# Head norms of a recurrence and a neighbourhood attention: one Newton chain each, and k's columns first

## The chip, the cores and the metric

The kernel runs on one core of one Trainium2 chip. The metric is the device time of one execution in microseconds, as the median over several runs. Three runs of the kernel before took 2517.57, 2526.06 and 2529.08 us; the median is 2526.06.

## What is computed

The reference is a stack of blocks over 512 tokens of 1024 features (a gated recurrence with a convolution mixer, a conformer convolution, two cross attentions, two convolutional feed-forwards), then a second block: a mixer of two branches and a mixture of experts. The change lies in the second block's mixer:

```python
h = rmsnorm(x, norm1_g)
p = h @ w_in                                   # 1024 x 5504 columns
p_rwkv, q, k, v, gate_logits = split(p)
# branch 1: a recurrence in both directions over 8 heads of 64
p = p + mu_prev * (prev - p) + mu_next * (nxt - p)         # token shift
r, k, v, wl_f, wl_b, al_f, al_b, gl = split(p)
kk = heads(k * k_k)
kk = kk * rsqrt(sum(kk * kk, -1) + 1e-12)      # head norm of the recurrence's keys
# ... decays, rates, the state's recurrence, group norm, bonus
# branch 2: attention over a window of a 8 x 64 grid, 8 heads of 64
q = q * rsqrt(mean(q * q, -1) + 1e-6) * q_gain * 64 ** -0.5
k = k * rsqrt(mean(k * k, -1) + 1e-6) * k_gain
# ... scores with a bias, softmax, values
x = x + (g_a * y_a @ w_o_rwkv + g_b * y_b @ w_o_na) @ w_out
```

So there are three head norms: of the recurrence's keys, and of q and k of the attention. Each is a sum of squares over the 64 features of a head, for every token and head, then an inverse square root.

## The kernel before

Activations lie with features on the 128 partitions and the 512 tokens along the free axis; a tile of 128 x 512 holds two heads. Large products are made of 128 x 128 weight blocks. Each block is three matmuls of 512 columns (`mm3`, lines 524 to 526), because the weights and the activations are split into a rounded part and a rest: ScalarE rounds the weights (`whi`, L353) and VectorE or GpSimd takes the rest (`wlo`, L356). The blocks come from DRAM in chunks of 1 MB on SP's queue, in the order in which `plan` lists them, and `Stream.block` asserts that they are used in just that order. The accumulators in PSUM are five `acc` tiles and three `aux` tiles.

`w_in` has 43 column tiles of 128: 0 to 3 are r, 4 to 7 k and 8 to 11 v of the recurrence; 12 holds the decay's and 13 the rate's low-rank input, 14 the gate's; 15 to 18, 19 to 22 and 23 to 26 are q, k and v of the attention; 27 to 42 are the two branches' gates. `W_IN` (lines 83 to 92) lists them in the order of their computation. The first four (`AHEAD`) are accumulated together while the norm before them is still under way. The inner generator `columns` computes them one by one: it yields after the first four of a column's eight blocks (`begin`) and again when its epilogue is issued, so a column is two steps. A recurrence column is shifted (`shifted`: a multiply, a scaling on ScalarE and two scalar_tensor_tensor on VectorE) and kept in one of the tiles of `self.x`, whose own contents were written to DRAM just before. An attention column is multiplied by the token norm (L1241) and written to DRAM (`nq0` to `nv3`). A gate column goes through a tanh and to DRAM too.

The stages interleave by hand. First 10 steps of `columns` run. Then `prep` runs for the four pairs of heads p = 0 to 3: decays, products with the keys, Gram matrices. At each of its ten yields the strings `PREP` and `INVS` say how many steps of the columns and of `inverse(0)` are issued in between. Then `inverse(1)` runs with columns (`SOLVE`) and pieces of the attention (`NEAR`). Last come the 32 slots of the recurrence (`chunk`, eight chunks for each pair), between which `GATE` and `REST` issue what is left of the columns and of the attention. Within these, each engine has a queue whose order is fixed when the program is built; a step that is not ready can be set behind a later one there, but on the chip each engine works through its own queue in order.

The head norms. `by_head` (L625) sums the squares of a tile for each head with four matmuls against a 128 x 2 selector, which gives a 128 x 8 tile with tokens on the partitions. `rsqrt` (lines 604 to 619) turns it into the inverse square root by a Newton iteration: a multiply-add, two integer operations for the first guess and three rounds of three instructions, 12 on VectorE, each on 128 x 8 and each waiting for the one before. `head_rms` does both and spreads the result back over the features (L635, eight matmuls). In `prep`, ScalarE scales the keys (L1402) and squares them (L1403); after the first yield `head_rms` follows and VectorE multiplies the keys by its result (L1473). In the attention's `start(p)`, once for each pair, q and k are read back from DRAM and squared (L1292, L1297); q's chain gives `rq` with one more instruction for the factor 0.125 (L1294), and k's goes through `head_rms` into the keys (L1300). `scores` uses `rq` as a scale for each token.

Of the kernel before, what the change touches and what calls it, by code (L numbers as in the profile page):

```python
# [8 lines left out]
F32 = mybir.dt.float32  # L9
F32R = mybir.dt.float32r  # L10
I32 = mybir.dt.int32
AF = mybir.ActivationFunctionType
ALU = mybir.AluOpType
# [3 lines left out]
P = 128  # L17
# [8 lines left out]
EPS = 1e-6  # L26
# [21 lines left out]
AHEAD = 4  # L48
# [31 lines left out]


OTHERS = list(range(15, 27)) + [14] + list(range(27, 43))
W_IN = [12, 13, 4, 0, 8]
for _p, _n in enumerate(BETWEEN):
    _h = [5 + _p, 1 + _p, 9 + _p] if _p < 3 else []
    _m = len(_h) + _n
    for _i in range(_m):
        if len(_h) and (_i + 1) * 3 // _m > _i * 3 // _m:
            W_IN.append(_h.pop(0))
        else:  # L90
            W_IN.append(OTHERS.pop(0))
W_IN += OTHERS


def plan():
# [52 lines left out]
    for m in (0, 8, 4, 12):  # L148
# [5 lines left out]
    blocks("w_in_2", 0, range(8),  # L154
           W_IN, AHEAD)
    blocks("w_o_na_2", 0, range(4), range(8))
# [288 lines left out]
class Kernel:  # L445
# [158 lines left out]
    def rsqrt(self, ps, n, scale, eps=EPS):  # L604
# [13 lines left out]
            r = o  # L618
        return r

    def by_head(self, sq):

        ps = self.aux()
        for j in range(4):
            self.nc.tensor.matmul(ps[:, 2 * j:2 * j + 2], sq[:, j * P:(j + 1) * P], self.c("sel"),  # L625
                                  start=True, stop=True)
        return ps[:, :8]

    def head_rms(self, sq, scale=1.0 / 64, eps=EPS):

        r = self.rsqrt(self.by_head(sq), 8, scale, eps)
        ps = self.aux()
        for j in range(4):
            for e, h in enumerate(HALF):
                self.nc.tensor.matmul(ps[h, j * P:(j + 1) * P],  # L635
                                      r[:, 2 * j + e:2 * j + e + 1].to_broadcast([P, 64]), self.idn,
                                      start=True, stop=True)
        return ps
# [496 lines left out]
    def final_norm(self):  # L1135


        nc = self.nc
        gf = self.v("final_norm", 0, DT)
        gg = self.C.tile([P, DT], F32, name="gg")  # L1140
        nc.vector.tensor_mul(gg, gf, self.v("norm1_g_2", 0, DT))
        xs = [self.split(t, scale=gg[:, i:i + 1]) for i, t in enumerate(self.x)]
        among = self.aheads(xs, "w_in_2", 0, range(8), (12, 13, 4, 0))
        for _ in range(6):
            next(among)
        r = self.rsqrt(self.by_token(*self.total(self.x, True, ends=ENDS)), 4, 1.0 / D)

        q = self.M.tile([P, 8], F32, name="rs", bufs=12)[:, :4]
        u = self.M.tile([P, 8], F32, name="rs", bufs=12)[:, :4]
        nc.vector.tensor_mul(q, r, r)  # L1150
        nc.vector.tensor_mul(u, q, self.by_token(*self.total(self.x, True, gf, ENDS)))
        r2 = self.rsqrt(u, 4, 1.0 / D)
        rr = self.M.tile([P, 8], F32, name="rs", bufs=12)[:, :4]
        nc.vector.tensor_mul(rr, r, r2)
        for _ in among:
            pass
        rb = self.M.tile([P, S], F32, name="rb", bufs=2)
        nc.vector.tensor_copy(rb, self.spread(rr))
        rx = self.M.tile([P, S], F32, name="rb", bufs=2)
        nc.vector.tensor_copy(rx, self.spread(r))  # L1160
        for i, t in enumerate(self.x):
            nc.vector.scalar_tensor_tensor(t, t, gf[:, i:i + 1], rx, op0=ALU.mult, op1=ALU.mult)
        return xs, rb
# [16 lines left out]
    def columns(self):  # L1180


        nc = self.nc
        R = self.R
        xs, rb = self.final_norm()
# [31 lines left out]
            return dst  # L1217

        kept = {}

        def columns():
            for m in W_IN:
                begin(m)
                yield
                if m < 12:
                    n, i = "rkv"[m // 4], m % 4
                    kept[n, i] = shifted(m, self.x["krv".index(n) + 3 * (i % 2)])
                elif m == 12:
                    w = shifted(m, self.tmp())
                    self.wl = R.tile([P, S], F32, name="wl")  # L1230
                    nc.scalar.activation(self.wl, w, AF.Tanh)
                elif m == 13:
                    self.al = shifted(m, R.tile([P, S], F32, name="al"))
                elif m == 14:
                    g = shifted(m, self.tmp())
                    nc.scalar.activation(g, g, AF.Tanh, scale=0.5)
                    nc.vector.tensor_scalar(g, g, 0.5, 0.5, op0=ALU.mult, op1=ALU.add)
                    self.put("gl", g, nc.scalar)
                elif m < 27:
                    t, ps = self.tmp(), col(m)  # L1240
                    nc.vector.tensor_mul(t.rearrange("p (c r) -> p r c", r=8),  # L1241
                                         ps.rearrange("p (r c) -> p r c", r=8),
                                         rb.rearrange("p (r c) -> p r c", r=8))
                    self.put("n%s%d" % ("qkv"[(m - 15) // 4], (m - 15) % 4), t)
                else:
                    t = self.tmp()
                    nc.vector.tensor_mul(t, col(m), rb)

                    nc.scalar.activation(t, t, AF.Tanh, bias=self.hg[:, m - 27:m - 26], scale=0.5)
                    self.put(f"gate{m - 27}", t, nc.scalar)  # L1250
                yield

        todo = columns()
        for _ in range(10):
            next(todo)
        inv = iter(())
        at = 0
# [17 lines left out]
    def neighbours(self):  # L1275

        nc = self.nc
# [8 lines left out]
        def start(p):  # L1286
            own = self.B.tile([P, 8, 320], F32, name="ab", bufs=2).rearrange("p a b -> p (a b)")
            q, k, v, *vs = (own[:, i * S:(i + 1) * S] for i in range(5))
            for n, t in (("nq", q), ("nk", k), ("nv", v)):
                self.get(f"{n}{p}", t)  # L1290
            sq = self.tmp()
            nc.scalar.activation(sq, q, AF.Square)  # L1292
            rq = self.M.tile([P, 8], F32, name="rq")
            nc.vector.tensor_scalar(rq, self.rsqrt(self.by_head(sq), 8, 1.0 / 64), 0.125, None,  # L1294
                                    op0=ALU.mult)
            sk = self.tmp()
            nc.scalar.activation(sk, k, AF.Square)  # L1297
            rk = self.head_rms(sk)
            kn = k
            nc.vector.scalar_tensor_tensor(kn, k, self.gqk, rk, op0=ALU.mult, op1=ALU.mult)  # L1300
            vt = []
# [80 lines left out]
    def prep(self, p, k, r, v):  # L1382

        nc = self.nc
        R, T, M = self.R, self.tmp, self.M
        Copy = AF.Copy
        rev = lambda t, d: t[:, ::-1] if d else t
        by = lambda t: t.rearrange("p (c s) -> p c s", s=64)
        lo, up = HALF
        q = p % 2  # L1390
# [6 lines left out]
        nc.sync.dma_start(wup, self.a["lora"][0, :, p * P:(p + 1) * P])  # L1397
        aup = M.tile([P, P], F32, name="wup", bufs=2)
        nc.sync.dma_start(aup, self.a["lora"][1, :, p * P:(p + 1) * P])

        kk, sq = T(), T()
        nc.scalar.activation(kk, k, Copy, scale=self.v("k_k_2", p))  # L1402
        nc.scalar.activation(sq, kk, AF.Square)  # L1403
        decays, rates, kd, abs_ = [], [], [], []

        def decay(d):
# [62 lines left out]

        decay(0)  # L1470
        yield
        rk = self.head_rms(sq, 1.0, 1e-12)
        nc.vector.tensor_mul(kk, kk, rk)  # L1473
        decay(1)
        yield
        products(0)
# [17 lines left out]
        for d in range(2):  # L1494
# [7 lines left out]
            t = T()  # L1502
            nc.scalar.copy(t, ps)
            t = t.rearrange("s (j i) -> s j i", j=4)
# [660 lines left out]
```

## Time and profile before

| | profiled execution |
|---|---|
| its own time | 2533.4 us |
| span of the profile | 2531.6 us |
| mean granted clock of TensorE | 0.965 of full speed |
| TensorE (PE) busy | 2421.6 us, 96% of the span |
| VectorE (DVE) busy | 1446.3 us, 57% |
| ScalarE (ACT) busy | 931.6 us, 37% |
| GpSimd (POOL) busy | 455.3 us, 18% |
| chain that ended last | PE 82%, DVE 10%, the rest 8% |

[...] A wait is given as the instruction that waited, an arrow, and what released it. The stages that the change touches lie between about 1570 and 2100 us of the span: the columns ahead of `prep` to about 1597, `prep` from there to 1757, the inverse to about 1885 and the recurrence's slots after it.

### The profile page before, as it was taken

To read this page: it belongs to the slowest core of one execution; us is meant where nothing else is said; L and a number is where in the kernel's file an instruction comes from. 1 tells how busy PE (TensorE), PEld (TensorE's weight loads), DVE (VectorE), ACT (ScalarE), POOL (GpSimd) and SP (SyncE) were. 2 spreads that over 40 slices of the span, in tenths; PEclk is the share of its full clock that TensorE was granted. 3 is DMA by queue.
4 is the path that set the end of the run, shared out by engine and by line. 5 is a ranking of instruction groups with operands and counts; after the bars stand their busy time and mean duration, and the time that the engine had idled before them with its cause. 6 is when DMAs were issued, how large, how long until landed. Compare 5 with 4: busy or idle time off the path is not lost.

```text
span 2531.6 us, 34476 instructions
## 1 busy us (share of the span) xinstructions
PE 2421.6 (96%) x13101; PEld 1863.7 (74%) x13101; DVE 1446.3 (57%) x2839; ACT 931.6 (37%) x1666; POOL 455.3 (18%) x428
## 2 busy tenths in 40 slices
PE   7999999999999999999999999898989999999996
PEld 6887888888887788888888887666777767764441
DVE  8988656444445456656445446788556776631110
ACT  4666444333333245444333334433233332321110
POOL 2112111110011000101110015343213320402211
PEclk9999999999999999999999999988879999989999
DMA  5332212222232213212322223445553344379998
GB/s 184 122 117 100 84 67 88 100 100 96 87 104 94 84 67 129 88 66 93 100 100 86 97 100 122 125 131 139 156 143 108 100 137 137 125 256 364 371 377 298
DMA packets 131195, 344.50 MB, mean 136 GB/s; under 512 B 40435, under 2 KB 66834, under 8 KB 101328
## 3 DMA queue, kind: packets, MB, share of 16 engines
q1 hardware_dynamic: 122944, 327.29, 37.9%
q0 software_dynamic: 5632, 10.49, 2.3%
q10 hardware_dynamic: 2448, 4.46, 0.5%
q8 instruction: 105, 1.72, 0.3%
q14 instruction: 66, 0.54, 0.1%
HBM read 307.33 MB, written 34.87 MB: 135 GB/s over the span
## 4 chain that ended last, share of the span: by engine, by line
PE 82%; DVE 10%; issue 2%; DMA 2%; ACT 2%; POOL 1%; SPq 0%; POOLq 0%; DVEq 0%; ACTq 0%
PE acc L524 20%; PE acc L525 20%; PE acc L526 20%; PE acc L2011 4%; PE aux L1995 3%; PE acc L2038 2%; DVE wlo L356 1%; PE acc L1612 1%; DMA raw<-wex 1%; PE aux L635 1%; DVE z L1529 1%; PE aux L592 1%; PE aux L1320 1%; DVE rs L615 1%; PE aux L1633 1%
## 5 line engine op out<-in xcount | busy, mean ns | idle before, releaser
L353 ACT CAST whi<-raw 128x512 fp32r<-128x512 f32 x652 | 398.6, 620 | 765.6 <-PE acc L525 641.2
L524 PE MATMUL acc<-xn,whi 128*128 128x512 f32 x1656 | 662.9, 401 | 12.6 <-ACT xn L562 6.6
L526 PE MATMUL acc<-xn,wlo 128*128 128x512 f32 x1656 | 658.3, 398 | 3.8 <-DVE wlo L356 3.8
L525 PE MATMUL acc<-xn,whi 128*128 128x512 f32 x1656 | 660.2, 399 | 0.0
L356 DVE TENSOR_TENSOR wlo<-raw,whi 128x512 fp32r<-128x512 f32 x605 | 446.4, 743 | 304.8 <-ACT whi L353 302.8
L524 PEld LDWEIGHTS acc<-xn,whi 128*128 128x128 f32 x1656 | 317.2, 192 | 84.4 <-ACT xn L562 6.6
L526 PEld LDWEIGHTS acc<-xn,wlo 128*128 128x128 f32 x1656 | 317.1, 192 | 72.6 <-DVE wlo L356 4.7
L525 PEld LDWEIGHTS acc<-xn,whi 128*128 128x128 f32 x1656 | 317.4, 192 | 72.0 <-issue 6.2
L524 PE MATMUL acc<-act,whi 128*128 128x512 f32 (+1 forms) x676 | 254.1, 377 | 3.1 <-DVE tmp L1761 1.8
L525 PE MATMUL acc<-act,whi 128*128 128x512 f32 (+1 forms) x676 | 254.0, 376 | 2.2 <-DVE act L560 2.2
L526 PE MATMUL acc<-act,wlo 128*128 128x512 f32 (+1 forms) x676 | 253.9, 376 | 0.0
L698 POOL TENSOR_TENSOR tmp<-tmp 128x512 f32<-128x512 f32 x48 | 74.3, 1549 | 628.0 <-DVE tmp L696 560.9
L582 POOL TENSOR_TENSOR tmp<-tmp 128x512 f32<-128x512 f32 x56 | 80.5, 1437 | 422.5 <-ACT tmp L575 404.0
L524 PEld LDWEIGHTS acc<-act,whi 128*128 128x128 f32 x676 | 128.1, 190 | 28.9 <-DVE tmp L1761 2.3
L525 PEld LDWEIGHTS acc<-act,whi 128*128 128x128 f32 x676 | 128.1, 190 | 27.6 <-DVE act L560 2.6
L526 PEld LDWEIGHTS acc<-act,wlo 128*128 128x128 f32 x676 | 128.1, 190 | 25.1
L560 DVE TENSOR_TENSOR act<-tmp,act 128x512 fp32r<-128x512 f32 x88 | 61.1, 695 | 87.1 <-ACT act L559 85.1
L559 ACT CAST act<-tmp 128x512 fp32r<-128x512 f32 x88 | 54.4, 620 | 122.2 <-POOL tmp L698 91.2
L2043 POOL DMA_INDIRECT out<-tmp,tid x32 | 50.7, 1583 | 246.3 <-ACT tmp L2042 156.5
L356 POOL TENSOR_TENSOR wlo<-raw,whi 128x512 fp32r<-128x512 f32 x47 | 63.8, 1360 | 138.8 <-ACT whi L353 119.9
L678 DVE SCALAR_TENSOR_TENSOR tmp<-tmp,vec 128x512 f32<-128x512 f32 x96 | 72.1, 752 | 17.1 <-ACT tmp L675 15.3
L2011 PE MATMUL acc<-raw,xn 128*64 128x512 f32 x320 | 75.8, 602 | 4.5 <-DMA raw<-wex 4.4
(425 smaller groups left out, 3364.4 us busy)
## 6 DMA issues: line engine op xcount, KB each, us to landing
raw<-wst SPq DMA_DIRECT2D x162, 1024.0 KB, 5.0
raw<-wex SPq DMA_DIRECT2D x56, 1024.0 KB, 16.0
whi<-wex SPq DMA_DIRECT2D x56, 256.0 KB, 7.1
wlo<-wex SPq DMA_DIRECT2D x56, 256.0 KB, 6.0
x<-wex SPq DMA_DIRECT2D x12, 1024.0 KB, 9.8
bkv<-bkv SPq DMA_DIRECT2D x32, 192.0 KB, 2.5
rec<-ab SPq DMA_DIRECT2D x8, 512.0 KB, 3.8
sp_gate<-tmp ACTq DMA_DIRECT2D x16, 256.0 KB, 2.1
```

Source lines behind the costliest of these rows:

```text
L353: self.nc.scalar.copy(hi, raw)
L356: rest.tensor_sub(lo, raw, hi.bitcast(F32))
L524: nc.tensor.matmul(ps, w[0], x[0], start=first, stop=False)
L525: nc.tensor.matmul(ps, w[0], x[1], start=False, stop=False)
L526: nc.tensor.matmul(ps, w[1], x[0], start=False, stop=last)
L559: nc.scalar.copy(h, src)
L560: nc.vector.tensor_sub(lo, src, h.bitcast(F32))
L582: nc.gpsimd.tensor_add(n, accs.pop(), t)
L678: nc.vector.scalar_tensor_tensor(z, h[:, k:k + S], taps[k], y, op0=ALU.mult, op1=ALU.add)
L698: nc.gpsimd.tensor_mul(z, u, ge)
L1995: nc.tensor.matmul(ps[:, k * 256:(k + 1) * 256], x[:, j * P:(j + 1) * P], self.at[g][j // 2][:, j % 2], start=n + j == 0, stop=n * 4 + j == 7)
L2011: nc.tensor.matmul(pg[a], h[:, o:o + SLOTS], w[2 * k + n], start=c + k == 0, stop=c + k == 4)
```

## The change

Three things change. `W_IN` has the recurrence's keys (4 to 7) ahead of its first r and v, and the number of steps that run before `prep` follows from the position of column 8: 16 instead of 10, so eight columns instead of five. The two steps that make sums of squares move into `columns`: `collect` squares a key or an attention column as soon as it is there, sums by head and lets ScalarE copy the 128 x 8 result into a shared tile. The new `rsqrts` runs the same Newton iteration once over 32 columns after the last of the keys, and once over 64 columns after the last of the attention's k; the factor 0.125 of q lies in the scale and the epsilon of its half. `prep` and `start` then only spread their slice. The scaling of the keys by `k_k` becomes the scalar of the squaring and of the multiply.

```diff
-W_IN = [12, 13, 4, 0, 8]
+W_IN = [12, 13, 4, 5, 6, 7, 0, 8]
 for _p, _n in enumerate(BETWEEN):
-    _h = [5 + _p, 1 + _p, 9 + _p] if _p < 3 else []
+    _h = [1 + _p, 9 + _p] if _p < 3 else []
...
+    def rsqrts(self, t, n, scales):
+        nc = self.nc
+        x, q, r, a, b = (t[:, i * n:(i + 1) * n] for i in range(5))
+        for c, scale, eps in scales:
+            nc.vector.tensor_scalar(q[:, c], x[:, c], scale, eps, op0=ALU.mult, op1=ALU.add)
+        nc.vector.tensor_scalar(a.bitcast(I32), q.bitcast(I32), 1, None, op0=ALU.arith_shift_right)
+        nc.vector.tensor_scalar(r.bitcast(I32), a.bitcast(I32), -1, 0x5f3759df, op0=ALU.mult,
+                                op1=ALU.add)
+        for _ in range(3):
+            nc.vector.tensor_mul(a, r, r)
+            nc.vector.scalar_tensor_tensor(b, a, -0.5, q, op0=ALU.mult, op1=ALU.mult)
+            nc.vector.scalar_tensor_tensor(r, b, 1.5, r, op0=ALU.add, op1=ALU.mult)
+        return r
...
     def head_rms(self, sq, scale=1.0 / 64, eps=EPS):
-        r = self.rsqrt(self.by_head(sq), 8, scale, eps)
+        return self.spread_heads(self.rsqrt(self.by_head(sq), 8, scale, eps))
+
+    def spread_heads(self, r):
         ps = self.aux()
...
+        sums = R.tile([P, 5, 32], F32, name="sums").rearrange("p a b -> p (a b)")
+        self.nsums = self.B.tile([P, 5, 64], F32, name="nsums").rearrange("p a b -> p (a b)")
+
+        def collect(t, to, at, scale=1.0):
+            sq = self.tmp()
+            nc.scalar.activation(sq, t, AF.Square, scale=scale)
+            nc.scalar.copy(to[:, 8 * at:8 * at + 8], self.by_head(sq))
...
-                    kept[n, i] = shifted(m, self.x["krv".index(n) + 3 * (i % 2)])
+                    at = i if n == "k" else 4 + "rv".index(n) + 2 * (i % 2)
+                    kept[n, i] = shifted(m, self.x[at])
+                    if n == "k":
+                        collect(kept[n, i], sums, i, self.v("k_k_2", i))
+                    if m == 7:
+                        self.rk = self.rsqrts(sums, 32, [(slice(0, 32), 1.0, 1e-12)])
...
+                    if m < 23:
+                        collect(t, self.nsums, m - 15)
+                    if m == 22:
+                        self.rn = self.rsqrts(self.nsums, 64, [(slice(0, 32), 1.0, 64 * EPS),
+                                                               (slice(32, 64), 1.0 / 64, EPS)])
...
-        for _ in range(10):
+        for _ in range(2 * W_IN.index(8) + 2):
             next(todo)
...
-            sq = self.tmp()
-            nc.scalar.activation(sq, q, AF.Square)
-            rq = self.M.tile([P, 8], F32, name="rq")
-            nc.vector.tensor_scalar(rq, self.rsqrt(self.by_head(sq), 8, 1.0 / 64), 0.125, None,
-                                    op0=ALU.mult)
-            sk = self.tmp()
-            nc.scalar.activation(sk, k, AF.Square)
-            rk = self.head_rms(sk)
+            rq = self.rn[:, 8 * p:8 * p + 8]
+            rk = self.spread_heads(self.rn[:, 32 + 8 * p:40 + 8 * p])
...
-        kk, sq = T(), T()
-        nc.scalar.activation(kk, k, Copy, scale=self.v("k_k_2", p))
-        nc.scalar.activation(sq, kk, AF.Square)
+        kk = T()
...
-        rk = self.head_rms(sq, 1.0, 1e-12)
-        nc.vector.tensor_mul(kk, kk, rk)
+        nc.vector.scalar_tensor_tensor(kk, k, self.v("k_k_2", p),
+                                       self.spread_heads(self.rk[:, 8 * p:8 * p + 8]), op0=ALU.mult,
+                                       op1=ALU.mult)
```

With the order of the columns the step strings now reach other ones: the fillers of prep 0 are 1, 9, 15, 2 (before: 15, 5, 1, 9), of prep 1 are 10, 16, 3, 11 (16, 6, 2, 10), of prep 2 are 17 to 20 (17, 7, 3, 11) and of prep 3 are 21 to 26 (18 to 23). Twelve steps of gate columns are left for the recurrence's slots, where there were eighteen; they end in slot 14 instead of 21, counted from 0, and the attention's pieces in slot 21 in both.

## Rows read from the trace of the kernel before

**Rows 1.** busy time by stretch: us, each engine's busy us, granted clock, DMA share, GB/s
```profile
1583.30:1597.00 13.70, 11.95 (x34) 7.22 (x32) 10.14 (x23) 6.56 (x11) 2.02 (x2) 0.75 0.28 90
1597.00:1660.00 63.00, 55.02 (x319) 39.62 (x318) 51.94 (x91) 26.02 (x42) 28.97 (x25) 0.91 0.50 134
1660.00:1689.00 29.00, 27.12 (x119) 18.89 (x118) 19.73 (x44) 12.04 (x20) 8.75 (x11) 0.79 0.47 135
1689.00:1757.00 68.00, 58.87 (x325) 43.21 (x325) 65.59 (x133) 23.40 (x39) 27.94 (x23) 0.88 0.47 128
1994.00:2064.00 70.00, 69.88 (x710) 49.82 (x709) 55.57 (x169) 26.69 (x75) 21.35 (x43) 1.00 0.32 97
2064.00:2096.00 32.00, 28.48 (x317) 21.91 (x318) 22.64 (x79) 4.81 (x15) 7.04 (x18) 0.73 0.47 149
```

**Rows 2.** waits, 1580 to 1765 us: who <- for whom: total us, times, longest
```profile
PE aux L635 <- DVE rs L617: 9.8, 4, 4.7
...
PE aux L1458 <- DVE ab L1443: 7.4, 6, 2.1
...
PE aux L1409 <- ACT wl L1231: 1.7, 1, 1.7
```

**Rows 3.** waits on TensorE's queue, 1800 to 2000 us, in the same form
```profile
PE aux L635 <- DVE rs L617: 6.2, 4, 2.2
...
PE aux L625 <- ACT tmp L1292: 1.2, 1, 1.2
```

**Rows 4.** the rs tile's instructions alone, by stretch (columns as in rows 1, without GpSimd)
```profile
1580.00:1765.00 185.00, 6.07 (x64) 4.91 (x64) 17.08 (x48) 0.00 (x0) 0.86 0.48 131
1765.00:2100.00 335.00, 5.81 (x64) 4.55 (x64) 19.74 (x100) 0.00 (x0) 0.89 0.42 127
```

**Rows 5.** timeline of VectorE around prep 0's chain: start us, us, engine, line, operation
```profile
1601.19 0.17 DVE L617 SCALAR_TENSOR_TENSOR rs<-rs 128x8 f32<-128x8 f32 x1
1601.40 1.19 DVE L615 TENSOR_TENSOR rs<-rs 128x8 f32<-128x8 f32 x1
...
1605.28 0.69 DVE L1473 TENSOR_TENSOR tmp<-tmp,aux 128x512 f32<-128x512 f32 x1 [1.28 <-PE aux L635]
```

**Rows 6.** timeline of GpSimd in the same stretch
```profile
1601.37 1.19 POOL L1439 TENSOR_TENSOR ab<-x,tmp 128x512 f32<-128x512 f32 x1 [4.25 <-ACT tmp L1423]
```

**Rows 7.** timeline of VectorE, 1694 to 1696 us, an instruction of 60 columns
```profile
1695.16 0.20 DVE L1529 TENSOR_TENSOR z<-X,NT 128x60 f32<-128x60 f32 x1
```

**Rows 8.** timeline of TensorE in column 8: starts one block of three apart
```profile
1578.07 0.39 PE L524 MATMUL acc<-xn,whi 128*128 128x512 f32 x1
...
1578.75 0.39 PE L524 MATMUL acc<-xn,whi 128*128 128x512 f32 x1
```

**Rows 9.** five lines by source: count, ns min/median/max, first and last start, shape
```profile
L1213 DVE SCALAR_TENSOR_TENSOR tmp<-tmp,vec x15: 736/750/1351, 1581.6 to 1831.4; 128x512 f32<-128x512 f32 x15
...
L1241 DVE TENSOR_TENSOR tmp<-acc,rb x12: 1071/1117/1178, 1609.1 to 1807.6; 128x512 f32<-128x512 f32 x12
...
L1402 ACT ACTIVATE tmp<-x,vec x4: 706/710/712, 1590.9 to 1716.3; 128x512 f32<-128x512 f32 x4
...
L1403 ACT ACTIVATE tmp<-tmp x4: 627/630/636, 1595.7 to 1717.1; 128x512 f32<-128x512 f32 x4
...
L1662 ACT COPY x<-aux x16: 212/213/213, 1894.6 to 2020.8; 128x64 f32<-128x64 f32 x16
```

**Rows 10.** timeline of VectorE, 2066 to 2091 us: rh copies, one per slot
```profile
2070.35 0.28 DVE L1629 COPY rh<-aux 128x128 f32<-128x128 f32 x1
...
2074.05 0.28 DVE L1629 COPY rh<-aux 128x128 f32<-128x128 f32 x1
...
2084.23 0.29 DVE L1629 COPY rh<-aux 128x128 f32<-128x128 f32 x1
...
2090.33 0.29 DVE L1629 COPY rh<-aux 128x128 f32<-128x128 f32 x1
```

**Rows 11.** timeline of TensorE, 2078 to 2080 us, with the idle time before
```profile
2078.64 0.92 PE L1612 MATMUL acc<-w,bkv 64*128 64x128 f32 x6 [1.84 <-DMA w<-rec]
```

More of the change, by code (lines that the diff above doesn't have):

```diff
@@ L1142, in final_norm @@
         xs = [self.split(t, scale=gg[:, i:i + 1]) for i, t in enumerate(self.x)]
-        among = self.aheads(xs, "w_in_2", 0, range(8), (12, 13, 4, 0))
+        among = self.aheads(xs, "w_in_2", 0, range(8), W_IN[:AHEAD])
         for _ in range(6):
@@ L1385, in prep @@
         R, T, M = self.R, self.tmp, self.M
-        Copy = AF.Copy
         rev = lambda t, d: t[:, ::-1] if d else t
```

## The prediction

> **What bounds the kernel now.** I read the page's busy lines first (the table ahead): TensorE is busy for 96% of the span, so time is lost where it waits or where its clock is low. Second the table by stretch [rows 1], to see where that is. In the preparation of the recurrence (1597 to 1757 us) TensorE is busy for 55.0 of 63, 27.1 of 29 and 58.9 of 68 us, at granted clocks of 0.91, 0.79 and 0.88; in the third stretch VectorE is busy 65.6 of 68 us and is the bound beside it. In 1994 to 2064 us, where attention pieces and gate columns fill the recurrence's gaps, TensorE is full (69.9 of 70, clock 1.00). In 2064 to 2096 us, where these fillers have run out, it is busy for 28.5 of 32 at clock 0.73.
> Third the list of waits [rows 2, 3]. The largest item on TensorE's own queue in the preparation is the spread matmul (L635) waiting for the Newton chain (rs, L617): 9.8 us in four waits. The Gram matmuls wait 7.4 us for VectorE's products (ab). In the attention the same spread waits 6.2 us, in four. Fourth VectorE's timeline around one chain [rows 5]: a chain is 12 instructions on 128x8, each 0.17 us when alone; then the spread, and the key's multiply (L1473) comes 1.28 us later.
>
> **Terms of the sum**, against the profiled execution: span 2531.6, 1.8 around it, 2533.4 in all; this is 7.3 above the median of 2526.06, and the difference is carried over to that median.
>
> *Chains.* Before there are 4 chains for keys and 8 for attention, with 4 scalings by 0.125: 148 instructions, busy 17.08 + 19.74 = 36.8 us [rows 4]. After there are 2 chains of 12 and 13, on 128x32 and 128x64. The nearest row is 128x60 at 0.20 us [rows 7]: 25 x 0.20 = 5 us. So VectorE is relieved of about 32 us. The low bound: 148 x 0.165 = 24.4, the rest of the 36.8 being time in which a tiny instruction took over 1 us. The row shows why: the one at 1601.40 took 1.19 us, beside GpSimd's multiply of the same length [rows 5, 6]. If the next VectorE instruction inherits that stall, the relief is 24.4 - 5 = 19 us.
> [...]
> I count neither figure as time, since VectorE bounds only the one stretch. What lies on the path is TensorE's wait for the chain. After the change the spread reads a result made long before, so the wait goes: **-9.8 us** in preparation, **-6.2** in attention [rows 2, 3]. What is late next: the products' 7.4 us, which I leave as they are. VectorE can follow, since it loses more than TensorE gains: in prep 3 the chain goes, and prep 2's fillers are columns 17 to 20 instead of 17, 7, 3, 11, that is three token-shift epilogues (a multiply, 0.69 like L1473, and two at 0.75: 2.2 us [rows 5, 9]) for plain ones at 1.12 [rows 9], 3.2 us less. The attention's one chain (13 x 0.20 = 2.6 us) lands in prep 3. Bounds of this term: 0 (products take over all of it) to -16.0.
>
> *Three columns ahead of prep(0).* 16 generator steps run instead of 10, so columns 4 to 7, 0 and 8 precede. A block of three matmuls takes 0.68 us [rows 8]; a column has 8 blocks, so three columns move 16.3 us of TensorE work from the end of the gate columns to the front. The work is the same, and so are its weight transfers. At the front it covers TensorE's wait for the decay's input (L1409, **-1.7 us** [rows 2]) in a stretch where TensorE was busy 12.0 of 13.7 us at clock 0.75 [rows 1]. I give no further gain there, since VectorE has eight epilogues to do in that place. At the end three columns of filler are missing. In 1994 to 2064 TensorE would have 69.9 - 16.3 = 53.6 us left; VectorE 55.6 less about 4 for three gate epilogues and their weights' remainders, 51.6. So the 70 us can shrink to 54 at best; with the recurrence's own waits I take 60, which gives back 10 of the 16.3: **+6 us**. Bounds: 0, and 16.3 if nothing is given back.
>
> *Clock.* What the low clock took in the three preparation stretches is 0.09 x 63 + 0.21 x 29 + 0.12 x 68 = 20 us [rows 1]. The chain's waits are 9.8 of the 17.2 us that chain and products make TensorE wait, which would be 11 us of it; products' waits stay close by, so I take half, **-6 us**. Bounds 0 and -11.
>
> *At nothing.* Squares: 12 before and after (four keys, eight attention tiles), and so are their by-head matmuls. Four ScalarE scalings of k go, and twelve copies of 128x8 from PSUM come; nearest row 128x64 at 0.21 us [rows 9], 2.6 us in all. ScalarE hides them, busy 26 of 63 us [rows 1]; with no cover they would cost those 2.6 us. The key's multiply becomes one instruction with a scalar, of the same shape. SP: eight spills of x stand ahead of the weights as before; the keys now write x0 to x3, whose spills go out first, so I expect no wait. Attention's q and k are still written to and read from DRAM. New waits: each by-head matmul in the columns stands on TensorE's queue behind its column's epilogue; that is the slower rival below. Attention's one wait of this kind was 1.2 us [rows 3].
>
> Sum: -9.8 - 6.2 - 1.7 - 6 + 6 = -17.7 us: 2533.4 becomes 2515.7, and the median 2526.1 becomes **2508**.
>
> **Rivals.**
> *Given back.* VectorE's products set the preparation, so the chain's 9.8 us come back as longer waits of the Gram matmuls, and the clock stays: -6.2 - 1.7 + 6 = -2, **2524**. For it: VectorE 65.6 of 68. Against: chain and three epilogues leave that very stretch.
> [...]
> *By-head matmuls stall the columns; slower.* TensorE works in order. A key's square needs the column's last matmul, then 0.69 + 0.71 + 0.75 + 0.75 + 0.71, about 3.6 us on VectorE and ScalarE; attention's q and k need 1.12 + 0.63 = 1.75 [rows 9]. Were each by-head matmul queued right behind its own column, 4 x 3.6 + 8 x 1.75 = 28 us of waits, and no clock gain: -17.7 + 6 + 28 = +17, **2543**. It decides from about 1 us of wait per by-head matmul. Against: the order written into the queues sets these matmuls behind other work, with the one 1.2 us wait.
> *More.* All chain-bound clock returns and the tail gives everything back: -16.0 - 1.7 - 11 = -29, **2497**.
> That the change does not do what it says I exclude: chains fall from 12 to 2 by the code.
>
> **Chances.** Forecast 0.42, given back 0.18, tail 0.12, by-head stalls 0.13, more 0.15. A median here tells no less than about 0.5% (12.6 us) from no change. Faster by over that: 0.42 + 0.15, less 0.04 for a forecast that falls short: 0.53. Within: 0.18 + 0.04 + 0.05 of the tail: 0.27. Slower: 0.13 + 0.07: 0.20. The range 2488 to 2541 reaches from the last rival with some 9 us for the measurement to just short of the stalls; the forecast's own is 2500 to 2516.
>
> **What would show it.** Right: no wait of L635's spread for rs in preparation and attention; rs instructions on VectorE near 25 there, under 7 us; TensorE's clock above 0.90 in preparation; the Gram matmuls' wait for ab near 7 us; gate columns ending about three columns earlier; the stretch with the last attention pieces some 10 us shorter. Wrong: ab waits grown by the 10 us that rs lost; waits of L625 for ScalarE's squares in the columns above 10 us in sum; bare slots at 6 us from the middle of the recurrence on, with clock near 0.5.

## The result

The changed kernel takes 2509.43 us in the median of five runs (2502.3 to 2518.14), the kernel before 2526.06; the ratio is 0.9933, with a 95% interval of 0.9913 to 0.9954. That is 17 us faster; forecast were 18. In the profiled execution the span falls from 2531.6 to 2507.7 us.

By stretch, after (us, busy us of PE, PEld, DVE, ACT and POOL with counts, granted clock, DMA share, GB/s). The first is the end of the columns ahead, the next four are `prep`, the last three the second half of the recurrence's slots; they answer to [rows 1].

```profile
1574.00:1603.00 29.00, 27.61 (x137) 22.83 (x135) 22.46 (x45) 12.95 (x23) 6.66 (x5) 1.00 0.43 151
1603.00:1642.00 39.00, 34.03 (x196) 24.61 (x196) 32.90 (x60) 17.55 (x30) 14.84 (x11) 0.96 0.50 124
1642.00:1680.00 38.00, 33.50 (x197) 24.75 (x195) 27.13 (x43) 16.24 (x28) 19.79 (x22) 0.91 0.56 139
1680.00:1720.00 40.00, 34.34 (x201) 25.64 (x201) 34.46 (x65) 14.79 (x27) 13.91 (x11) 0.87 0.49 130
1720.00:1767.00 47.00, 40.53 (x228) 30.90 (x227) 39.71 (x79) 15.97 (x30) 21.05 (x18) 0.89 0.51 133
...
1980.00:2015.00 35.00, 33.67 (x352) 24.37 (x350) 29.45 (x89) 16.46 (x49) 10.97 (x24) 1.00 0.36 106
2015.00:2050.00 35.00, 32.38 (x292) 24.27 (x293) 22.57 (x78) 6.35 (x21) 7.12 (x19) 0.61 0.16 45
2050.00:2080.00 30.00, 25.29 (x350) 19.24 (x350) 24.80 (x88) 4.77 (x14) 7.04 (x18) 1.00 0.51 164
```

The waits on TensorE's queue from 1560 to 1770 us, answering to [rows 2]: L641 is the by-head matmul, L653 the spread, L1485 the Gram matmuls.

```profile
PE aux L641 <- ACT tmp L1244: 13.0, 7, 4.8
PE aux L1485 <- DVE ab L1470: 8.0, 3, 4.5
...
PE aux L1485 <- DVE go L1490: 0.9, 1, 0.9
...
PE aux L653 <- DVE sums L634: 0.4, 1, 0.4
```

The spread's 9.8 us are down to 0.4, and in the attention (1760 to 2100 us) there is none left of the 6.2 of [rows 3]. The wait for the products has not grown much, from 7.4 to 8.0. A new one has come, 13.0 us in seven by-head matmuls. The chains' instructions, by tile, answer to [rows 4]: the keys' tile and the attention's.

```profile
1580.00:1770.00 190.00, 4.37 (x64) 3.44 (x64) 2.37 (x12) 0.66 (x4) 0.92 0.50 134
```

```profile
1580.00:1770.00 190.00, 0.00 (x0) 0.00 (x0) 2.73 (x13) 1.32 (x8) 0.92 0.50 134
```

148 instructions of 36.8 us became 25 of 2.37 + 2.73 = 5.1 us.

Stage by stage, between the first and the last instruction of the same lines, profiled executions before and after: `prep` (first to last decay matmul, L1409 before, L1436 after) 152.3 and 131.1 us; from there to the end of the inverse 142.8 and 144.9; from there to the last slot 243.6 and 224.0; the next 104 us are the same in both. The first decay matmul comes 17.7 us later (1585.4, 1603.1), which is the three columns (16.3) and a little more. So 17.7 + 2.1 are paid and 21.2 + 19.6 won; the remaining 2.9 us of the 23.9 lie behind these stages. The second gain compares with 16.2 us in the forecast (10 for columns that leave the slots, 6.2 for the chains' waits), and what carries it is the subject of the first four experiments.

### The profile page after: what moved, and what is told of

Read it like the earlier page. It is cut to its first block, busy times and chain, and to the rows that moved or that the text cites. A ratio compares the mean times of both kernels' runs of the same rounds, so it can differ in the third digit from the quotient of the medians.

```text
span 2507.7 us, 34375 instructions
## 1 busy us (share of the span) xinstructions
PE 2401.0 (96%) x13101; PEld 1860.4 (74%) x13101; DVE 1427.4 (57%) x2716; ACT 930.0 (37%) x1674; POOL 457.8 (18%) x428
## 5 line engine op out<-in xcount | busy, mean ns | idle before, releaser
L524 PE MATMUL acc<-xn,whi 128*128 128x512 f32 x1656 | 660.7, 399 | 13.1 <-ACT xn L562 6.5
L525 PE MATMUL acc<-xn,whi 128*128 128x512 f32 x1656 | 655.9, 396 | 0.0
L524 PEld LDWEIGHTS acc<-xn,whi 128*128 128x128 f32 x1656 | 315.7, 191 | 84.7 <-ACT xn L562 6.5
L525 PEld LDWEIGHTS acc<-xn,whi 128*128 128x128 f32 x1656 | 316.1, 191 | 67.8 <-issue 2.5
L524 PE MATMUL acc<-act,whi 128*128 128x512 f32 (+1 forms) x676 | 252.6, 374 | 3.1 <-DVE tmp L1789 1.8
L525 PE MATMUL acc<-act,whi 128*128 128x512 f32 (+1 forms) x676 | 252.2, 373 | 2.7 <-DVE act L560 2.7
L524 PEld LDWEIGHTS acc<-act,whi 128*128 128x128 f32 x676 | 129.9, 192 | 25.7 <-DVE tmp L1789 2.2
L525 PEld LDWEIGHTS acc<-act,whi 128*128 128x128 f32 x676 | 129.8, 192 | 25.6 <-DVE act L560 3.5
```

The lines of the kernel that those rows point to most:

```text
L524: nc.tensor.matmul(ps, w[0], x[0], start=first, stop=False)
L525: nc.tensor.matmul(ps, w[0], x[1], start=False, stop=False)
```

## The experiments

Every ratio is against the kernel before, run beside it on the same chip (its medians there are 2523.02, 2526.45 and 2525.05 us); where kernels from different chips are compared I compare their ratios and turn the difference into us at 2526.

**The parts one by one.** The change has three parts: the order of the columns, the keys' chain and the attention's chain. The keys' chain needs the order; the other combinations can be run.

*The order alone.* The kernel before, with all its twelve chains:

```diff
-W_IN = [12, 13, 4, 0, 8]
+W_IN = [12, 13, 4, 5, 6, 7, 0, 8]
...
-    _h = [5 + _p, 1 + _p, 9 + _p] if _p < 3 else []
+    _h = [1 + _p, 9 + _p] if _p < 3 else []
...
-        for _ in range(10):
+        for _ in range(2 * W_IN.index(8) + 2):
```

> The kernel before with the new order of columns and 16 steps ahead of prep alone; all twelve chains stay where they were. If the chains are what pays (theory of the prediction), the order alone is worth -1.7 us of covered wait and +6 us of missing filler in the last slots: about +4, 2530 us, and the spread still waits near 16 us for rs. If the order is what pays (rival: eight columns ahead of prep cover its latencies), most of the gain is here already: 2509 to 2513 us.

*The order and the keys' chain,* with the attention's own eight chains kept in `start`:

```diff
+                    if n == "k":
+                        collect(kept[n, i], sums, i, self.v("k_k_2", i))
+                    if m == 7:
+                        self.rk = self.rsqrts(sums, 32, [(slice(0, 32), 1.0, 1e-12)])
```

> The new order and the one chain for the recurrence's keys; the attention keeps its own eight chains. Theory of the prediction: -9.8 -6 -1.7 +6 = -11.5, 2514.5 us, with the attention's spread waiting about 6 us for rs. If the by-head matmuls of the attention's columns, which in the changed kernel wait 13.0 us for their squares, cost what they wait, leaving them out here outweighs the 6.2 us: 2502 us.

*The attention's chain alone,* in the old order:

```diff
+                    if m < 23:
+                        collect(t, self.nsums, m - 15)
+                    if m == 22:
+                        self.rn = self.rsqrts(self.nsums, 64, ...)
...
-            rq = self.M.tile([P, 8], F32, name="rq")
-            nc.vector.tensor_scalar(rq, self.rsqrt(self.by_head(sq), 8, 1.0 / 64), 0.125, None, ...)
+            rq = self.rn[:, 8 * p:8 * p + 8]
```

> The kernel before with the attention's one chain alone: old order of columns, four chains for keys. Theory of the prediction: -6.2, 2520 us. If the waits of the by-head matmuls for squares cost their full time: -6.2 + 13, 2533 us. If only the order pays: 2526 us.

*The order and the attention's chain,* with the keys' four chains kept: the edit of the first on top of the third.

> The kernel before with the new order of columns and the attention's one chain, but with the keys' four chains kept. It fills the last corner: the order alone stood at 2563.5, the order with the keys' chain at 2541.7, all three at 2509.4. [...] Rival (the two mergings only work together): 2550 or more.

| order | keys' chain | attention's chain | median us | ratio, 95% interval | slots us, clock there |
|---|---|---|---|---|---|
| | | | 2526.06 | 1 | 243.6, 0.91 |
| x | | | 2563.53 | 1.0158 (1.0128 to 1.0189) | 247.6, 0.80 |
| x | x | | 2541.73 | 1.0083 (1.0061 to 1.0105) | 240.0, 0.84 |
| | | x | 2527.04 | 1.0021 (1.0007 to 1.0035) | 237.0, 0.91 |
| x | | x | 2520.46 | 0.9997 (0.9978 to 1.0016) | 216.9, 0.95 |
| x | x | x | 2509.43 | 0.9933 (0.9913 to 0.9954) | 224.0, 0.90 |

Both sides' numbers for the first two were far off: the order alone costs 40 us, not 4, and with the keys' chain the time is 2541.73, not 2514.5 or 2502. The third came out at the 2526 of "only the order pays", though the order does not pay either. The keys' chain is worth the same wherever it can be tried: 1.0083 - 1.0158 is -19 us, 0.9933 - 0.9997 is -16. The attention's chain is not: without the order it is worth nothing (+5 us), with it 1.0158 to 0.9997, -41 us, and 1.0083 to 0.9933, -38. Put the other way, the order costs 40 us while the attention's eight chains stand, and -6 (1.0021 to 0.9997, intervals overlapping) once they are one. My theory for the fourth run was that the attention's chain does this whatever the keys do, since it takes the two pauses away that its pairs of chains leave in the recurrence; that gave slots near 225 us and 2527 to 2537 in all. It held for the slots (247.6 to 216.9 us); the total came out below, and the pauses as the reason are looked at next.

Most of this is in the slots: the fourth run's are 30.7 us shorter than those of the order alone, the changed kernel's 16.0 shorter than those with the order and the keys' chain. Part is in the inverse, which the attention's one chain shortens by 5.8 and 9.5 us in the new order (151.2 to 145.4, 154.4 to 144.9). VectorE's timeline in the kernel before, from one slot's rh copy to the next one's, with `start(2)` between them:

```profile
1915.39 0.29 DVE L1629 COPY rh<-aux 128x128 f32<-128x128 f32 x1 [0.52 <-PE aux L1626]
...
1919.93 0.17 DVE L609 TENSOR_SCALAR rs<-aux 128x8 f32<-128x8 f32 x1 [0.34 <-PE aux L625]
...
1923.94 0.17 DVE L609 TENSOR_SCALAR rs<-aux 128x8 f32<-128x8 f32 x1
...
1930.37 1.25 DVE L616 SCALAR_TENSOR_TENSOR rs<-rs 128x8 f32<-128x8 f32 x1
1931.65 0.17 DVE L617 SCALAR_TENSOR_TENSOR rs<-rs 128x8 f32<-128x8 f32 x1
1933.57 0.75 DVE L1300 SCALAR_TENSOR_TENSOR ab<-ab,gqk,aux 128x512 f32<-128x512 f32 x1 [1.75 <-PE aux L635]
1936.30 0.29 DVE L1629 COPY rh<-aux 128x128 f32<-128x128 f32 x1 [1.98 <-PE aux L1626]
```

The same two slots after:

```profile
1921.76 0.29 DVE L1657 COPY rh<-aux 128x128 f32<-128x128 f32 x1 [0.48 <-PE aux L1654]
1929.88 0.29 DVE L1657 COPY rh<-aux 128x128 f32<-128x128 f32 x1 [0.79 <-PE aux L1654]
```

Two chains, one after the other, and the spread behind them stand between two slots: 20.9 us, where after the change there are 8.1. A second such pause (20.0 us against 8.5) is at `start(3)`. The slots next to a pause are shorter than they are after the change, though (5.2 and 4.5 us), so the pauses are weighed by longer stretches: the ten slots from the fourth rh copy to the fourteenth, which hold both pauses, and the eighteen from there to the last copy. For the kernel before, the order alone, the fourth run and the changed kernel, in this order:

```profile
1915.40:2003.60 88.20, 84.48 (x793) 62.87 (x793) 62.42 (x209) 31.18 (x91) 23.84 (x47) 0.96 0.36 115
2003.60:2124.10 120.50, 116.86 (x1108) 83.46 (x1108) 85.01 (x268) 35.04 (x91) 27.70 (x57) 0.92 0.36 113
```

```profile
1940.50:2029.30 88.80, 84.20 (x799) 63.04 (x799) 64.40 (x211) 32.55 (x94) 24.35 (x47) 0.96 0.34 107
2029.30:2154.00 124.70, 115.68 (x1030) 85.14 (x1030) 79.44 (x261) 26.80 (x78) 22.53 (x53) 0.69 0.30 91
```

```profile
1933.40:2010.90 77.50, 77.08 (x745) 54.24 (x745) 53.62 (x156) 29.79 (x88) 23.14 (x45) 1.00 0.39 120
2010.90:2115.10 104.20, 94.65 (x1053) 68.94 (x1054) 78.58 (x265) 28.67 (x81) 23.56 (x56) 0.98 0.36 110
```

```profile
1913.70:1991.20 77.50, 77.07 (x745) 54.20 (x745) 53.58 (x156) 29.78 (x88) 23.10 (x45) 1.00 0.38 120
1991.20:2103.10 111.90, 103.36 (x1053) 75.13 (x1053) 79.11 (x264) 28.68 (x81) 23.44 (x56) 0.88 0.33 103
```

The attention's one chain takes 11 us out of the ten slots (8 beside the keys' chain, where they took 85.3), and it does so in the old order too (76.9 us in the third run). The new order does not make the pauses longer or emptier: the ten slots take 88.2 and 88.8 us, with TensorE idle for 3.7 and 4.6 us and the clock at 0.96 in both. What the order alone loses lies in the eighteen slots behind. They have three columns (16.3 us) less to do than before and yet take 4 us more, at a clock of 0.69 instead of 0.92. The slots of the order alone, as a whole and from 2040 to 2110 us:

```profile
1906.40:2154.00 247.60, 228.44 (x2062) 168.15 (x2061) 162.89 (x524) 68.00 (x197) 60.44 (x135) 0.80 0.33 103
```

```profile
2040.00:2110.00 70.00, 65.37 (x540) 49.30 (x540) 42.82 (x137) 14.43 (x46) 14.11 (x34) 0.50 0.23 67
```

TensorE's granted clock is 0.50 of full speed for these 70 us on end, and TensorE is idle in short pieces that make 4.6 us of the 70. What 0.50 means for one matmul the changed kernel shows: of one kind, 128x512, they start 0.43 us apart at 1699.4 to 1700.7 us, where the clock is 0.50, and 0.23 us apart at 1705.2 to 1705.9 us, where it is 1.00. The low stretch, the time on end at 0.50 in the later slots, for the order alone, the order with the keys' chain, and the changed kernel:

```profile
2038.60:2117.10 78.50, 72.77 (x614) 54.98 (x614) 48.24 (x157) 15.98 (x49) 16.49 (x40) 0.50 0.27 82
```

```profile
2017.80:2079.20 61.40, 57.26 (x465) 42.98 (x466) 37.70 (x121) 13.27 (x42) 11.19 (x28) 0.50 0.15 43
```

```profile
2022.30:2049.60 27.30, 25.29 (x210) 19.20 (x208) 15.84 (x54) 5.46 (x18) 4.79 (x12) 0.50 0.16 45
```

In the first two it begins where the gate columns end (the last one's tanh starts at 2038.6 and 2018.9 us), 18 to 19 us after the second pause. The slots with the attention's chain merged too (fourth run) keep a clock of 0.95, and only 3.4 us behind their last gate column are at 0.50:

```profile
1898.20:2115.10 216.90, 201.15 (x2031) 143.87 (x2030) 151.63 (x474) 67.21 (x194) 60.05 (x136) 0.95 0.38 117
```

That the clock goes with the loss shows in the other executions too. Over the 17 runs of the kernel before beside it the span falls by 18 us for each 0.01 of mean granted clock; the order alone had 0.954 in the mean against 0.970, which by that slope is an estimated 30 of the 39 us between the means. With the keys' chain the mean is 0.960, in the fourth run 0.966.

So two things are shown. The merged chain of the attention shortens the ten slots with the pauses by 8 to 11 us in either order, and in the new order the low stretch behind them is short with it (27.3 and 3.4 us) and long without it (78.5 and 61.4, one profiled execution each). Why the second goes with the first is not shown. The pauses lie before the low stretch, TensorE is idle in them for at most 1 us more than before, and no run took the pauses away without merging the chains.

**Three columns given back to the slots.** The theory was that pauses without filler cost the clock; then the same edit must help where they are and not where they are gone. For the changed kernel I took columns in the slots as free and in the inverse as paid in full, 2493 to 2500 us; for the kernel with the pauses, where the columns were to fill them, 2528 to 2536, with the clock in the slots at 0.90 or more instead of 0.84. Six of the 22 gate steps that `SOLVE` issues during the inverse are left for the slots: in the changed kernel, and in the kernel with the order and the keys' chain only.

```diff
-SOLVE = "10110001011011100011010101010110101010200"
+SOLVE = "10010001001010100010010100010100101010200"
```

> The changed kernel with three of the gate's columns (six of the 22 gate steps that the solve's schedule issues) left for the recurrence's slots, which then hold as many gate columns as in the kernel before: 18 half-column steps instead of 12. [...] Rival (with both chains merged the slots have no pause left, so TensorE bounds them and the columns are paid wherever they stand): 16 us shorter solve, 16 us longer slots, total 2505 to 2512.

> The kernel with the new order and the keys' one chain, the attention's own chains kept, with three of the gate's columns left for the slots (16 gate steps in the solve instead of 22). The same step made the changed kernel 9 us slower (2509.4 to 2518.5): there the slots had no pause left and the columns were paid in full. [...] Rival (columns are paid in the slots wherever they are put): slower, 2548 to 2553.

The changed kernel became slower, 2518.46 us (0.9967, 0.9951 to 0.9983), by about 9 us with intervals that just touch; it lies above both the theory (2493 to 2500) and the rival (2505 to 2512). Its inverse and slots (144.9 and 224.0 us without the edit):

```profile
1734.10:1875.00 140.90, 122.81 (x1004) 100.84 (x1002) 84.49 (x177) 42.30 (x84) 33.27 (x27) 0.83 0.52 148
1875.00:2112.60 237.60, 227.91 (x2104) 159.22 (x2102) 157.95 (x480) 72.23 (x203) 64.35 (x139) 0.91 0.37 115
```

The kernel that still has the pauses became faster, 2534.81 us (1.0033, 1.0016 to 1.0050) from 2541.73, by about 13 us, as its theory had it. Its inverse and slots (154.4 and 240.0 without the edit):

```profile
1735.10:1880.90 145.80, 127.60 (x1017) 103.61 (x1015) 87.92 (x213) 43.56 (x84) 30.81 (x27) 0.82 0.50 142
1880.90:2120.60 239.70, 227.55 (x2135) 164.51 (x2134) 166.66 (x530) 74.86 (x207) 64.87 (x139) 0.92 0.36 114
```

The same three columns (16.3 us of TensorE) cost the slots 13.6 us without pauses and -0.3 with them, where the clock went from 0.84 to 0.92. Where they land, though, is behind the pauses. In the kernel that has them the ten slots stay (85.3 and 86.5 us) and the eighteen behind take 118.8 us instead of 120.2 with the columns in them, the low stretch being 17.1 us instead of 61.4. In the changed kernel the eighteen grow from 111.9 to 126.0, the low stretch being 23.9 instead of 27.3. So the columns paid for themselves where the low stretch had been long and became short, and cost nearly all of their time where it was short before. That prices filler; it does not show that the pauses bring the clock down. In the inverse they are worth only 4.0 and 8.6 us either way: taken out there, TensorE waits instead (18.1 us of 140.9 idle, 8.6 before the edit) at a clock of 0.83 instead of 0.88.

**The by-head matmuls.** The changed kernel with the attention's eight by-head matmuls and copies issued one column later:

```diff
-            nc.scalar.copy(to[:, 8 * at:8 * at + 8], self.by_head(sq))
+            if to is sums:
+                nc.scalar.copy(to[:, 8 * at:8 * at + 8], self.by_head(sq))
+            else:
+                waiting.append((sq, to[:, 8 * at:8 * at + 8]))
...
                     t, ps = self.tmp(), col(m)
+                    settle()
...
-                    if m == 22:
+                    if m == 23:
```

`settle` issues the by-head matmuls and copies that wait; the attention's chain moves one column later with them.

> The changed kernel with the attention's by-head matmuls issued one column later, behind the next column's matmuls; the squares stay where they are. If their 13.0 us of waiting are time lost: 2497 us, and the waits fall under 3 us. If TensorE would only wait for the products instead (the Gram matmuls stand behind them in the same stretches): the waits of the Gram matmuls grow by as much, and the time stays at 2509 us.

It ran in 2496.32 us, ratio 0.9923 (0.9892 to 0.9953); by ratio that is 2.5 us below the changed kernel, and the two intervals can't be told apart. Its median says less than the ratio here: four of its six times lie at 2495 to 2497 us, two near 2511.6. Its waits in the same stretch:

```profile
PE aux L1494 <- DVE ab L1479: 11.3, 4, 4.5
PE aux L1494 <- DVE go L1499: 3.9, 2, 3.6
...
PE aux L641 <- DVE tmp L1508: 1.2, 1, 1.2
PE aux L641 <- ACT tmp L1244: 0.8, 1, 0.8
```

13.0 us became 2.0, but the products' waits rose from 8.9 to 15.2. Of the 13.0, 5.9 were in `prep`, which is as long as it was (132.5 us, 131.1 before the edit): there the wait moved to VectorE's products. Another 6.3 were in the inverse, which is 3.7 us shorter (141.2). The most that its profile gained was in the slots, 212.1 against 224.0 us, at a clock of 0.96 against 0.90. So my reading "stalls are time" is not shown. The same step in the kernel with the attention's chain alone:

```diff
+            waiting.append((sq, to[:, 8 * at:8 * at + 8]))
...
                     t, ps = self.tmp(), col(m)
+                    settle()
...
+                    if m == 23:
```

> The kernel before with the attention's one chain alone (its old order of columns and its keys' four chains kept), and with the by-head matmuls one column later than where the changed kernel has them. With them in the changed kernel's place this stood at 2527, 4 us above the kernel before. Theory (the merging is worth its 6 us or a little more and the stalls of the by-head matmuls ate it): 2512 to 2518. Rival (in the old order the pauses of the recurrence were covered by gate columns, so the merging is worth nothing there): 2522 to 2527.

2527.85 us (1.0002, 0.9983 to 1.0021): the rival's side. In the old order the attention's chain is worth nothing by the medians even without the stalls. In its profile, as in the third run's, the ten slots are 11.3 us shorter than before and the eighteen behind 4.9 (5.3 there) longer, so the slots as a whole gain 6.9 (6.6).

**What is left of the chains.** Nine Newton rounds instead of three in both merged chains, 36 instructions more:

```diff
-        for _ in range(3):
+        for _ in range(9):
```

> The changed kernel with nine Newton rounds instead of three in each of the two merged chains: 18 more small VectorE instructions per chain, 36 in all, near 0.2 us each, about 3.5 us more per chain. It prices what is left of the chains. Theory (the merged chains end long before their first reader): 0 to +2 us, 2509 to 2511. Rival (the merged chain still stands on the path, behind it the products that the Gram matmuls wait for, or the copies that free PSUM): +3.5 to +7 us, 2513 to 2517.

2519.91 us (0.9960, 0.9938 to 0.9982), 7 us above the changed kernel, though the two intervals overlap. `prep` took 136.6 us instead of 131.1 and the inverse 151.5 instead of 144.9, so the rival is nearer. The first spread now waits for the keys' chain itself, 0.4 us before the edit:

```profile
PE aux L653 <- DVE sums L634: 2.9, 1, 2.9
```

Whether the rest comes through products that stand behind the chains on VectorE is not shown.

**Better versions.** With the by-head matmuls late, two ways to keep filler for the slots: the three columns given back, two steps ahead of the first slot, the rest even; or no column moved, only an even spread.

```diff
 # columns given back, SOLVE as above
+GATE = "01010110101011010101101010110000"
+REST = "11111111111111111111111111111212"
...
+                for _ in range(2):
+                    next(gates, None)
 # no column moved
+GATE = "00101010010101001010100101010000"
+REST = "11111111111111111111111111111212"
```

> The changed kernel with the attention's by-head matmuls one column later, the same three columns left for the slots, two gate steps issued ahead of the first slot, where the recurrence waits 4.6 us for its weights, and the remaining steps spread evenly over slots 0 to 27 rather than bunched. Theory (filler is free, the stalls of the by-head matmuls are real time): 2496 less up to 16, so 2480 to 2490, with the granted clock at 1.00 through the slots. Rival (columns are paid wherever they stand): 2494 to 2500, as with the by-head matmuls moved alone.

> The changed kernel with the attention's by-head matmuls one column later (2496.3) and, beyond that, the twelve gate steps and the attention's pieces that the slots issue spread evenly over slots 0 to 27 instead of bunched in the first half; no column is moved. Theory (TensorE's 7 to 8 us of idle time in slots 14 to 24 is there because the filler ran out by then, while the first half had more than it needed): 2487 to 2492, the slots near 205 us. Rival (the recurrence's own steps set each slot, and filler moved from the first half leaves the idle time there): 2494 to 2500.

The first took 2505.02 us (0.9907, 0.9884 to 0.9931), with the slots' clock at 0.97: slower than the theory (2480 to 2490) and the rival (2494 to 2500). The second took 2501.81 (0.9898, 0.9875 to 0.9920), the best ratio here. Its slots:

```profile
1880.30:2087.60 207.30, 201.23 (x2038) 142.13 (x2036) 156.66 (x477) 66.85 (x195) 61.51 (x137) 0.96 0.40 123
```

TensorE's idle time there fell from 13.7 us (212.1 - 198.4) to 6.1, as the theory said, and the slots were 4.8 us shorter. The total is above the theory's 2487 to 2492 and the rival's 2494 to 2500. By ratio it stands 9 us below the changed kernel, and within the interval of the version with the late matmuls alone.

## Why the prediction was right, and where it was not

**Right in sum, and in two groups of terms.** The keys' chain was -9.8 with a clock term of -6 in `prep`, together -15.8; measured are -16 and -19. (In the profiles `prep` is 25.7 and 27.3 us shorter by it and the columns ahead are 7.1 and 7.2 longer, since work moves across that boundary.) By an estimate from TensorE's busy time and its clock `prep` lost 135.9 x 0.12 = 16 us to the clock before and 115.8 x 0.08 = 9 after, so the clock's -6 was a -7. The order and the attention's chain together were -6.2 - 1.7 + 6 = -2; measured is 0.9997, -1.

**Wrong in how the second group is made up.** The prediction priced its two terms apart, as if they added up. They do not. The order's term was bounded by 0 and 16.3 us for columns not given back, and measures 40 when the attention's chains stay. The step that failed is "with the recurrence's own waits I take 60": it took the busy time of the stretch from 1994 us on, read at a clock of 1.00, and let the stretch shrink at that clock once its filler is gone. With the order alone the eighteen late slots do not shrink, since 78.5 us of them run at 0.50. The attention's -6.2 is there in the old order's slots (6.6 us), but not in its total (+5 and 0 us); in the new order the attention's chain is worth 38 to 41 us, because the low stretch is short with it. For the change as a whole the terms fit stage by stage: forecast were 16.3 us paid ahead of `prep`, 17.5 won by the keys' chain, its clock and the covered wait, and 16.2 in attention and slots; the profiles show 17.7, 21.2 and 17.5 (19.6 less the inverse's 2.1). That the two terms of this group nearly cancel as forecast is luck, since the prediction did not know that one needs the other.

**The tail starves.** The tail that starves, at 0.12 of the chances, had the low clock in slots without filler, but as a cost of 14 us in six late slots. That was an estimate of 6 x (6.1 - 3.7) from slots 3.7 us apart (clock 1.00) and 6.1 us apart (clock 0.50) in [rows 10], and it gave 2533 in all. The low clock is there in the changed kernel in part: clock 0.61 from 2015 to 2050 us, where 1994 to 2064 had 1.00 before [rows 1]. The order alone shows it in full, 78.5 us at 0.50. As its condition it had waits near 1.8 us per slot, from the 1.84 us of [rows 11]; that is not borne out by the waits just ahead of the fall: 1.53 us in the order alone, 0.38 in the changed kernel, and 2.28 in the fourth run, where the clock was at 0.50 for 3.4 us only. One line of each:

```profile
2037.51 0.66 PE L1358 MATMUL aux<-tmp,ab 128*64 128x128 f32 x8 [1.53 <-ACT tmp L1353]
```

```profile
2021.42 0.71 PE L1640 MATMUL acc<-w,bkv 64*128 64x128 f32 x6 [0.38 <-DMA w<-rec]
```

```profile
2074.63 0.71 PE L1639 MATMUL acc<-w,bkv 64*128 64x128 f32 x4 [2.28 <-DMA w<-rec]
```

**By-head matmuls at nothing.** The sign of the slower rival came, 13.0 us of waits, over its bound of 10, and the total stayed. Moving these matmuls handed 6.3 of the 11.0 us saved to the products and left `prep` as long. So the term stood, within what these runs can tell, though for another reason than "the order written into the queues sets these matmuls behind other work". That TensorE works in order shows at the longest of the waits: it stood idle for 4.82 us ahead of the by-head matmul at 1697.13 us, between the first matmul of a block (L524, 1691.91 us) and its second (L525, 1698.85 us), which reads the same `whi`.

**The signs.** rs and its successors took 5.1 us (under 7). `prep`'s clock was to be above 0.90: it is 0.96 and 0.91, then 0.87 and 0.89. Gate columns end at 1999 us instead of 2063, far more than three columns earlier. The slots shortened by 19.6 us: 10.7 in the ten that held the pauses (88.2 to 77.5) and 8.6 in the eighteen behind (120.5 to 111.9), where the prediction had some 10.

**The stall passed on.** The prediction left open whether small instructions that take over 1 us beside GpSimd's (1.19 us instead of 0.17 [rows 5, 6]) hand the stall on. The keys' twelve after the change take 2.37 us in all, 0.17 to 0.39 each, so none of them met it; VectorE's busy time fell by 1446.3 - 1427.4 = 19 us over the span, the lower of the two figures given (19 and 32). That does not settle it: records on VectorE overlap (in the kernel before one of 0.28 us starts at 1921.01 us, the next at 1921.21), and summed one by one they fall by 26 us, between the two. How much of a stall moves on to the next one no run here shows.

**Open.** Why the low stretch is long in the new order while the attention's chains stand, though they end before it begins, is open. Why the granted clock in the slots was 0.96 with late by-head matmuls and 0.90 without, at nearly the same idle time (13.7 and 14.4 us), is not settled. Nor is `prep` taken apart further: the waits point to VectorE's products, and no run shortened these alone.

## What to carry to other kernels

Taking filler out of the recurrence's slots had a price in clock that their busy time did not show: with the order alone and 16.3 us of matmuls less they took 4 us longer (247.6 against 243.6), at a clock of 0.80 instead of 0.91. Price the stretch behind the last filler at the low clock seen in the traces (0.50 here) as well as at the full one. Where a change has several parts, run them apart and in pairs: here one part costs 40 us without the other and nothing with it, which no single run would have told. A wait in the list is time only if nothing else fills or ends the stage: the keys' chain in `prep` was worth 16 to 19 us, the attention's nothing in the old order. Lengths between neighbouring slots misled here, since the slots beside a pause were shorter (5.2 and 4.5 us); compare stretches that hold both.

## What the runs showed of the hardware

TensorE can look busy and still be slow: in the order alone it is busy for 65.4 of 70 us with waits of 4.6 us in all, at 0.50 of full speed throughout; the low stretch lasted 78.5 us. The times of one kernel go with the clock: over the 17 runs of the kernel before on one chip the span went from 2512.2 us at a mean granted clock of 0.976 to 2530.2 at 0.966, with a correlation of -0.96 (-0.89 and -0.91 on the two other chips).
